# Attention in slots of four query blocks, with the value products of two groups in one block of the array

## The chip, the core and the metric

The kernel runs on one core of a Trainium2 chip. A core has five engines that run at the same time, each in its own program order, and wait for one another through semaphores: TensorE (PE) for matrix products, VectorE (DVE), ScalarE (ACT) and GpSimd (POOL) for elementwise work, and SyncE (SP), which here issues most of the DMA transfers. PE reads its operands from SBUF and writes its results to PSUM, a small memory of eight banks; the other engines copy results out of PSUM. PE works in two steps, a weight load (PEld in the profile) and the matmul that streams columns past the loaded weights.

The metric is the device time of one execution in microseconds (us): the median over repeated runs.

## The reference

The reference is one decoder layer on a sequence of 4096 positions of width 1024. After an RMS norm and an input projection, two groups of heads work side by side, and their gated outputs go through one output projection, a residual add and a last RMS norm. What matters here is the first group: eight heads of width 64, each with three branches of sliding-window attention on the same q, k, v.

```python
DILATED_BRANCHES = ((128, 1), (512, 4), (2048, 16))   # window, dilation
...
s = jnp.einsum('bhrnqd,bhrnkd->bhrnqk', qb, kb) * (Dh ** -0.5)
...
s = jnp.where(mask, s, jnp.finfo(jnp.float32).min)
m = jnp.max(s, axis=-1, keepdims=True)
p = jnp.exp(s - m)
den = jnp.sum(p, axis=-1, keepdims=True)
o = jnp.einsum('bhrnqk,bhrnkd->bhrnqd', p.astype(v.dtype), vb) / den
```

With dilation d the sequence falls into d residues r, and each residue into blocks n of 128 queries. A block attends to its own 128 keys and to the 128 before it (none before block 0). So every branch has 32 blocks of 128 queries: 32 of one residue in branch 0, 8 each of four residues in branch 1, 2 each of sixteen in branch 2. The second group of heads is a retention in 32 chunks of 128 positions (scores with a decay, outputs from a running state, a group norm per head).

## The kernel before

The kernel has three stages. Stage 1 projects q, k, v and the retention's q and k. Stage 2 (`phase2`, the stage that the change touches) does the attention, and beside it the retention with its own value projection. Stage 3 does the gates and the output projection.

All five engines run the order in which the program was written (`manual_schedule`). In stage 2 two generators are woven into one order.

`attention()` goes through 192 groups, 24 per head, each of four query blocks (`head_groups`, from L375). A group's two pairs of blocks are its two *banks*. For a bank:

- `qk_bank` (L598): S, the scores of two blocks against 256 keys each, in one PSUM bank; four matmuls. Two S banks exist (`psS`). For branches 1 and 2, `gather_q` (L579) first copies the queries of a group together, half on DVE and half on POOL, two groups ahead.
- `row_max` (L632): on DVE, mask and row minimum of one block, in place in the S bank. The scores carry a minus sign, so the minimum serves as the maximum.
- `exp_row` (L640): on ACT, the exponential of one block into P, with the row sum.
- `t_bank` (L647): four transposes of P on PE into T; `t_copy` (L658) copies T to `pt`, bank 0 by DVE and bank 1 by ACT.
- `pv_ops`, `pv_group` (L666, L673): O, the values. The weights are 128 keys x 64 value columns, so one product fills half of the array's columns. Bank 0 of the group goes to one half, bank 1 to the other, in turn, and the two halves run side by side. The result is 64 rows x 256 columns in either half of one PSUM bank.
- `o_copy` (L695): on ACT, O to SBUF; `store_o` (L713) stores it by SP.

The loop (L766) runs in half groups t: S of bank t, transposes of the bank two half steps back, O of a group at every even t, then the ACT and DVE work. `later` and `issue_due` put stores and loads some half steps on.

`filler()` (L969) yields the retention's work in small parts, each with an estimated cost in ns. A chunk's value projection V has eight parts (k from 0 to 7) of three matmuls; between them come the retention's scores Rs, the transposes Rk of the decayed keys, the outputs Ro in two halves, the transposes Rt of the normalised output, and the next state Rkv, whose products are 64 columns wide like O's. `group_norm` (L930) puts DVE's normalising work beside V's parts: statistics at k=0, aggregate at 1, and at 4 and 5 two heads each, read from the bank (`psG`) into which the next Ro goes. `split_rk` (L848) prepares the next chunk at k=7.

The loop at the end of `phase2` weaves: after each half step it takes filler parts until the sum of costs reaches what is due by then (`slot`), so that the filler lasts until some steps (`TAIL`) before the end of the attention. When all values of V are done, stage 3's weights are loaded and split beside the rest (`early3`). Stage 3 begins with the scaling of its first block of inputs (`split_h`, L432 to L440), which needs a transfer of `rs`.

## Time and profile before

| | |
|---|---|
| time, median of 3 runs | 2446.45 us (2445.19 to 2449.05) |
| the profiled execution, its own time | 2448.65 us |
| span of its trace, first to last instruction | 2446.9 us |
| PE clock granted, mean | 0.986 of full |
| stage 2 in the trace, first S to last O | about 778 to 1682 us |
| O's matmul instructions (two per product) | 1968 |
| HBM read and written | 241.18 MB, 118.64 MB |

A row of the timeline gives start, duration, engine, line, operation, the tiles (out<-in), their shapes, and how many instructions of one kind were merged; in brackets the idle time of the engine before it, with what ended it. PE's matmuls are pipelined: their durations overlap, so their cost is read from start to start. A row of the groups by line gives the count, then the busy time in all and the mean of one in ns, then the idle time before them. A row of the waits gives who waited for whom, the time in all, how often, and the longest.

### The profile page before, as it was taken

The numbers are of one execution on the slowest core, as the hardware profiler recorded it, in microseconds if no ns is written. First come the engines' busy times: TensorE is split into PE (matmuls) and PEld (weight loads), VectorE is DVE, ScalarE is ACT, GpSimd is POOL, SyncE is SP. The second block draws the span as 40 slices with busy tenths as digits, with TensorE's granted clock in tenths as the row PEclk, the third lists the DMA queues.
The fourth block names the chain that finished last, engine by engine and source line by source line (L and its number), as shares of the span: only waits on it lengthen the run. The fifth ranks groups of instructions, "written<-read, shape, count | busy, mean of one in ns | idle before, by whom it ended". The sixth has DMA issues, their size and how long they took to land.

```text
span 2446.9 us, 41800 instructions
## 1 busy us (share of the span) xinstructions
PE 2343.5 (96%) x14568; PEld 1985.9 (81%) x14568; DVE 1485.2 (61%) x3921; ACT 989.6 (40%) x2868; POOL 714.3 (29%) x761
## 2 busy tenths in 40 slices
PE   7999999999995999999999999996899999999998
PEld 5778888888884888887888887885889889999997
DVE  5643443444342878787777879786665565565554
ACT  4322212212212666666666666666222232232221
POOL 5312112112102535343444435354312112121110
PEclk9999999999997999999999999998999999999999
DMA  6343344343348565758576665746675656676663
GB/s 189 129 148 120 124 139 132 113 137 129 120 146 208 138 163 137 178 130 190 132 165 153 154 158 127 169 118 197 149 162 153 146 158 154 150 156 165 141 158 91
DMA packets 404067, 362.59 MB, mean 148 GB/s; under 512 B 191784, under 2 KB 334760, under 8 KB 398736
## 3 DMA queue, kind: packets, MB, share of 16 engines
q1 hardware_dynamic: 389216, 332.91, 52.5%
q10 hardware_dynamic: 14112, 25.43, 3.3%
q8 instruction: 115, 1.88, 0.3%
q0 software_dynamic: 528, 1.58, 0.2%
q14 instruction: 96, 0.79, 0.1%
HBM read 241.18 MB, written 118.64 MB: 147 GB/s over the span
## 4 chain that ended last, share of the span: by engine, by line
PE 74%; DMA 10%; DVE 5%; issue 2%; ACT 2%; POOL 2%; SPq 1%; ACTq 0%; POOLq 0%; DVEq 0%
PE S L615 8%; PE mm L49 8%; PE mm L50 8%; PE mm L51 8%; PE O L685 6%; PE T L652 5%; PE po L49 3%; PE po L50 3%; PE po L51 3%; PE g L50 3%; PE g L49 3%; PE g L51 3%; PE V L49 3%; DMA wb<-dr_w 2%; PE V L51 2%; PE V L50 2%
## 5 line engine op out<-in xcount | busy, mean ns | idle before, releaser
L636 DVE CUSTOM_DVE_ANT_0 S<-S,mask 128x256 f32<-128x256 f32 (+1 forms) x768 | 308.5, 402 | 168.7 <-PE S L615 139.1
L643 ACT ACTIVATE P<-S,nm 128x256 f32<-128x256 f32 (+1 forms) x768 | 337.4, 449 | 74.4 <-DVE nm L636 51.2
L51 PE MATMUL g<-h,wg 128*128 128x256 f32 x1024 | 290.6, 284 | 0.0
L652 PE MATMUL T<-ident,P 128*128 128x128 f32 x1368 | 213.3, 273 | 0.4 <-ACT P L643 0.4
L615 PE MATMUL S<-kk,qc 128*128 128x256 f32 x1024 | 186.5, 306 | 17.1 <-ACT P L643 11.8
L50 PE MATMUL po<-wo,m 128*128 128x512 f32 x512 | 201.7, 394 | 0.0
L51 PEld LDWEIGHTS g<-h,wg 128*128 128x128 f32 x1024 | 197.6, 193 | 0.1
L685 PE MATMUL O<-pt,v 128*64 128x128 f32 (+1 forms) x1968 | 196.0, 325 | 0.2 <-ACT pt L662 0.2
L615 PEld LDWEIGHTS S<-kk,qc 128*128 128x128 f32 x1024 | 149.8, 190 | 45.5 <-issue 28.9
L41 ACT ACTIVATE m<-e 128x256 fp32r<-128x256 f32 x128 | 53.3, 417 | 323.9 <-DVE e L1123 171.7
L405 POOL TENSOR_TENSOR hc<-hr,hc 128x512 fp32r<-128x512 f32 x64 | 85.9, 1343 | 319.3 <-ACT hc L404 249.4
L49 PE MATMUL po<-wohi,m 128*128 128x512 f32 x448 | 175.7, 392 | 2.1 <-DVE x L1170 2.1
L1177 POOL TENSOR_TENSOR rs<-v,mhalf 128x1 f32<-128x1 f32 x32 | 17.3, 541 | 549.2 <-DVE v L1175 549.2
L51 PE MATMUL po<-wohi,m 128*128 128x512 f32 x448 | 176.4, 394 | 0.0
L159 POOL TENSOR_TENSOR sq<-sq,sq 128x512 f32<-128x512 f32 x56 | 76.2, 1361 | 326.8 <-ACT sq L155 326.8
L685 PEld LDWEIGHTS O<-pt,v 128*64 128x64 f32 x1968 | 121.4, 136 | 60.7 <-issue 31.0
L652 PEld LDWEIGHTS T<-ident,P 128*128 128x128 f32 x1368 | 163.7, 141 | 1.1 <-ACT P L643 1.1
L49 PE MATMUL g<-h,wg1hi 128*128 128x256 f32 x512 | 146.5, 287 | 14.2 <-ACT h L439 14.2
L643 ACT ACTIVATION_READ_ACCUMULATOR P<-S,nm 128x1 f32 x768 | 158.0, 206 | 0.0
L50 PE MATMUL g<-h,wg1hi 128*128 128x256 f32 x512 | 148.9, 291 | 2.2 <-DVE h L440 1.7
L49 PE MATMUL g<-h,wg0hi 128*128 128x256 f32 x512 | 145.0, 283 | 4.7 <-ACT e L1116 4.7
L50 PE MATMUL g<-h,wg0hi 128*128 128x256 f32 x512 | 144.8, 283 | 0.0
(207 smaller groups left out, 6097.9 us busy)
## 6 DMA issues: line engine op xcount, KB each, us to landing
hr<-in_xT_dram SPq DMA_DIRECT2D x64, 512.0 KB
q<-dr_q SPq DMA_DIRECT2D x128, 256.0 KB
wb<-dr_w SPq DMA_DIRECT2D x128, 192.0 KB
o<-dr_o SPq DMA_DIRECT2D x192, 128.0 KB
v<-dr_v SPq DMA_DIRECT2D x94, 256.0 KB
xt<-in_xT_dram SPq DMA_DIRECT2D x64, 256.0 KB
dr_q<-hl SPq DMA_DIRECT2D x32, 512.0 KB
dr_k<-hl SPq DMA_DIRECT2D x32, 512.0 KB
```

The lines of the kernel that those rows point to most:

```text
L41: nc.scalar.activation(dst[:, 0], src, AF.Copy)
L49: nc.tensor.matmul(out, wh, xh, start=first and i == 0, stop=False)
L50: nc.tensor.matmul(out, wh, xl, start=False, stop=False)
L51: nc.tensor.matmul(out, wl, xh, start=False, stop=last and i == n - 1)
L159: nc.gpsimd.tensor_tensor(sums[b], sums[b], sq, ALU.add)
L405: nc.gpsimd.tensor_tensor(hc[:, :, 1, :], src, hc[:, :, 0, :].bitcast(F32), ALU.subtract)
L615: nc.tensor.matmul(s[:, j * 256 : (j + 1) * 256], qq[h, t, half][:, off : off + 128] if br == 0 else it["q"][:, t, i, :], rhs, start=(j == ...
L636: nc.vector.tensor_tensor_reduce(sv, sv, mask[:, it["br"], c0:256], 1.0, BIG, ALU.add, ALU.min, accum_out=nm[:, col : col + 1])
L643: nc.scalar.activation(it["P", i // 2][:, i % 2, c0:256], sv, AF.Exp, bias=nm[:, col : col + 1], scale=-1.0, accum_out=den[:, col : col + 1])
L652: nc.tensor.transpose(t[:, j * 128 : (j + 1) * 128], it["P", bank][:, j // 2, j % 2 * 128 : j % 2 * 128 + 128], ident)
L685: nc.tensor.matmul(o[64 * bank : 64 * bank + 64, c0 : c0 + 128 * m], vt[h, br, idx // 8][:, idx % 8, :], it["pt"][:, a : a + m, :].rearran ...
L1177: nc.gpsimd.tensor_tensor(rs, v, mhalf, ALU.pow)
```

## The change

The attention now runs in slots of a whole group. In a slot g the PE order is: S of both banks of group g; filler parts marked "r"; the transposes of both banks of group g-1; filler parts marked "f"; and in odd slots the values of two groups, g-3 and g-2, in one block. Each of the two groups takes one half of the array's columns, with all its four blocks (64 rows x 512 columns in the bank). `pv_ops` now lists for every key block one product that serves its own queries and the next block's, where both are in the group.

The filler marks its parts by kind: V and Rs are "r", the others "f". The weaving takes parts of a kind only at that kind's place in the slot, and stops when the next part is of the other kind.

On DVE the four row minima of a group come in a row, on ACT its four exponentials. The copies of O cover two groups, so their count halves and their width doubles, and the stores' too. In branch 2 a group holds two neighbouring residues in place of two that lie four apart. There is one more buffer of P (4 for 3) and of `pt` (3 for 2), and the buffers for O's copy are twice as wide. The costs with which the weaving plans are set anew, and `TAIL` counts groups.

```diff
-TAIL = 8
+TAIL = 4
...
-    for r in (0, 1, 2, 3, 8, 9, 10, 11):
-        g.append((2, [(r, 0), (r, 1), (r + 4, 0), (r + 4, 1)]))
+    for r in (0, 4, 2, 6, 8, 12, 10, 14):
+        g.append((2, [(r, 0), (r, 1), (r + 1, 0), (r + 1, 1)]))
...
-        pp = pool("p2p", 3)
+        pp = pool("p2p", 4)
...
-        PT = [c2.tile([128, 8, 128], F32, name=f"pt{i}") for i in range(2)]
+        PT = [c2.tile([128, 8, 128], F32, name=f"pt{i}") for i in range(3)]
...
-        def pv_ops(it, bank):
-
-            r, n = it["blocks"][2 * bank]
-            s0 = 4 * bank
-            ops = [(r, n, s0 + 1, 2, 0), (r, n + 1, s0 + 3, 1, 128)]
-            return ([(r, n - 1, s0, 1, 0)] if n > 0 else []) + ops
+        def pv_ops(it):
+
+            ops, blocks = [], it["blocks"]
+            for i, (r, n) in enumerate(blocks):
+                if n > 0 and (r, n - 1) not in blocks:
+                    ops.append((r, n - 1, 2 * i, 1, i * 128))
+                ops.append((r, n, 2 * i + 1, 2 if (r, n + 1) in blocks else 1, i * 128))
+            return ops
...
-            ops = [pv_ops(it, bank) for bank in range(2)]
+            ops = [pv_ops(it) for it in pair]
             for x in range(-max(map(len, ops)), 0):
-                for bank in range(2):
+                for half in range(2):
...
-                ob = osp.tile([128, 256], F32, tag="os", name="os2")
-                nc.scalar.activation(ob, it["O"][:, :256], AF.Copy)
+                ob = osp.tile([128, 512], F32, tag="os", name="os2")
+                nc.scalar.activation(ob, o, AF.Copy)
                 c0 = n * 128 if br == 0 else r * 1024 + n * 128
-                later(2, store_o, h, br, c0, 512, ob)
+                later(2, store_o, h, br, c0, 1024, ob)
...
+            for g in range(n + 5):
+                clock[0] = 2 * g
                 issue_due()
-                it, b = half(t)
...
+                it, i1, i2 = item(g), item(g - 1), item(g - 2)
+                pair = items[g - 3 : g - 1] if g % 2 and 3 <= g < n + 2 else None
+                done = items[g - 4 : g - 2] if g % 2 == 0 and 4 <= g < n + 3 else None
...
+                if item(g + 2):
+                    gather_q(item(g + 2))
+                if done:
+                    o_copy(done)
+                cost = 0
                 if it:
-                    qk_bank(it, b)
-                    cost += 436
...
+                    for b in range(2):
+                        qk_bank(it, b)
+                    cost += 1030
+                if i2 and i2["gi"] == len(groups) - 1:
+                    end_head(i2["h"])
+                    cost += 2 * TRN
+                if it:
+                    for i in range(4):
+                        row_max(it, i)
+                    for i in range(4):
+                        exp_row(it, i)
+                rest = pv_cost(pair[1]) if pair else 0
+                yield "r", cost, rest + (t_cost(i1) if i1 else 0)
+                clock[0] = 2 * g + 1
+                issue_due()
                 if i1:
-                    exp_row(i1, 2 * b1)
-                    exp_row(i1, 2 * b1 + 1)
...
+                    for b in range(2):
+                        t_bank(i1, b)
+                        t_copy(i1, b)
+                yield "f", t_cost(i1) if i1 else 0, rest
+                if pair:
+                    pv_groups(pair)
+                yield "", rest, 0
...
                 for k in range(KT):
+                    yield ("r", 700) if c < NCH else ("f", 0)
...
                     if mid and k == 1:
+                        yield "r", 654
                         scores(mid)
                         decayed_q(mid)
-                        yield 654
                     if mid and k == 3:
+                        yield "f", 2 * TRN
                         decayed_k(mid)
-                        yield 2 * TRN
...
                         if mid:
+                            yield "f", 872
                             outputs(mid, 0)
-                            yield 872
                         if old:
+                            yield "f", 4 * TRN
                             ret_out(c - 2, old)
-                            yield 4 * TRN
                 if mid:
+                    yield "f", 872
                     outputs(mid, 1)
-                    yield 872
+                    yield "f", 478
                     next_state(mid)
-                    yield 478
...
+        for kind, cost, rest in attention():
             total += cost
-            while not values_done and total < (t + 1) * slot:
-                total += next(fg)
+            if not kind:
+                g += 1
...
+                continue
+            while not values_done and feed.next[0] == kind and total + rest < (g + 1) * slot:
+                total += feed.do()
```

The planner's due cost per slot, `slot`, is worked out as before from the costs of a head's groups and of the chunks' parts; a part's cost is now added when the part is done.

More of the change, by code (lines that the diff above doesn't have):

```diff
@@ L594, in gather_q @@
                     for n in range(2):
-                        src = qq[h, part, n].rearrange("p (m r) -> p r m", r=16)[:, r : r + 5 : 4, :]
+                        src = qq[h, part, n].rearrange("p (m r) -> p r m", r=16)[:, r : r + 2, :]
                         (nc.vector if part else nc.gpsimd).tensor_copy(t[:, part, n : n + 3 : 2, :], src)
@@ L685, in pv_group @@
                     nc.tensor.matmul(
-                        o[64 * bank : 64 * bank + 64, c0 : c0 + 128 * m],
+                        o[64 * half : 64 * half + 64, c0 : c0 + 128 * m],
                         vt[h, br, idx // 8][:, idx % 8, :],
-                        it["pt"][:, a : a + m, :].rearrange("p a b -> p (a b)"),
-                        start=-x == len(ops[bank]),
+                        pair[half]["pt"][:, a : a + m, :].rearrange("p a b -> p (a b)"),
+                        start=-x == len(ops[half]),
                         stop=x == -1,
@@ L1008, in filler, with __init__, do @@
                         if mid:
+                            yield "f", 872
                             outputs(mid, 0)
-                            yield 872
                         if old:
+                            yield "f", 4 * TRN
                             ret_out(c - 2, old)
-                            yield 4 * TRN
                 if mid:
+                    yield "f", 872
                     outputs(mid, 1)
-                    yield 872
+                    yield "f", 478
                     next_state(mid)
-                    yield 478
-        per_head = sum(
-            872 + TRN * (8 - sum(it["blocks"][2 * i][1] == 0 for i in range(2))) + pv_cost(it) for it in items[: len(groups)]
-        )
-        n = 2 * len(items)
-        slot = H * per_head / n + (NCH * (8250.0 + 6 * TRN) - LEAD - REST) / (n - TAIL)
+        class Feed:
+            def __init__(self):
+                self.parts = filler()
+                self.next = next(self.parts)
+            def do(self):
+                cost = self.next[1]
+                self.next = next(self.parts, None)
+                return cost
+        per_head = sum(1030 + t_cost(it) + (pv_cost(it) if i % 2 else 0) for i, it in enumerate(items[: len(groups)]))
+        n = len(items)
+        slot = H * per_head / n + (NCH * (8 * 700.0 + 3530.0) - LEAD - REST) / (n - TAIL)
         ctx.enter_context(tc.manual_schedule(engines=ORDERED))
-        fg = filler()
+        feed = Feed()
         total = 0.0
         while total < LEAD:
-            total += next(fg)
+            total += feed.do()
         total = 0.0
         gates = None
-        for t, cost in enumerate(attention()):
+        g = 0
+        for kind, cost, rest in attention():
             total += cost
-            while not values_done and total < (t + 1) * slot:
-                total += next(fg)
+            if not kind:
+                g += 1
+                if g == n - 4:
+                    ahead["h3"] = load_x_block(nc, qp, io, 0, soon)
+                continue
+            while not values_done and feed.next[0] == kind and total + rest < (g + 1) * slot:
+                total += feed.do()
             if values_done:
@@ L1040, in phase2 @@
                 for _ in range(2):
-                    next(fg, None)
+                    if feed.next:
+                        feed.do()
                 next(gates, None)
-            if t == n - 7:
-                ahead["h3"] = load_x_block(nc, qp, io, 0, soon)
-        assert not list(fg) and not list(gates)
+        assert not feed.next and not list(gates)
 def phase3(tc, io, dr, out, ahead, raw, M):
```

65 lines of the change are left out of this document (20 added, 45 removed).

## The prediction

> **What bounds the kernel now.** I read the page's head first, then the busy time by windows, then the timeline of the attention stage engine by engine, and the list of waits last.
>
> ```profile
> span 2446.9 us, 41800 instructions
> PE 2343.5 (96%) x14568; PEld 1985.9 (81%) x14568; DVE 1485.2 (61%) x3921; ACT 989.6 (40%) x2868; POOL 714.3 (29%) x761
> PE 74%; DMA 10%; DVE 5%; issue 2%; ACT 2%; POOL 2%; SPq 1%; ACTq 0%; POOLq 0%; DVEq 0%
> ...
> 778.00:1682.00 904.00, 873.90 (x6799) 730.24 (x6799) 707.53 (x2573) 602.87 (x2071) 402.30 (x455) 0.99 0.64 153
> ```
>
> The last row, of the windows, gives the length, the busy time of PE, weight loads, DVE, ACT and POOL, and the granted clock (0.99). The changed stage runs from 778 to 1682, 904 us for 192 groups, 4.7 us each. PE is busy for 97% of it and leads the chain of waits, DVE for 78%. So the PE order decides, and DVE stands close behind. What a busy row hides is seen in the starts on PE:
>
> ```profile
> 902.34 0.63 PE L615 MATMUL S<-kk,q 128*128 128x256 f32 x4
> 902.81 0.60 PE L652 MATMUL T<-ident,P 128*128 128x128 f32 x4
> ...
> 903.94 0.64 PE L615 MATMUL S<-kk,q 128*128 128x256 f32 x4
> 904.41 0.60 PE L652 MATMUL T<-ident,P 128*128 128x128 f32 x4
> ...
> 907.83 0.40 PE L49 MATMUL V<-w2hi,hc 128*128 128x512 f32 x1
> ...
> 908.52 0.64 PE L615 MATMUL S<-kk,q 128*128 128x256 f32 x4
> 909.00 0.60 PE L652 MATMUL T<-ident,P 128*128 128x128 f32 x4
> 909.53 1.09 PE L685 MATMUL O<-pt,v 128*64 128x128 f32 x12
> ...
> 911.12 0.60 PE L652 MATMUL T<-ident,P 128*128 128x128 f32 x4
> ```
>
> From start to start: four S take 904.41 - 903.94 = 0.47 us (0.117 each); three V (two rows left out) take 908.52 - 907.83 = 0.69; four T and three V take 903.94 - 902.81 = 1.13, so four T 0.44, 0.109 for 128 columns. Between these kinds nothing is lost. With an O in between, 909.00 to 911.12 is 2.12 us for four T, twelve O and four S. The twelve O are six on either column half, side by side, and stream eight times 128 columns per half: 0.87 at the pace of T. What is left, 2.12 - 0.44 - 0.47 - 0.87 = **0.34 us**, is what going to the 64-column form (the 128*64 in the row) and back costs, once per group, 192 times.
>
> **The change, part by part.** *Values of two groups at once.* An O block now holds two groups, one per half. Columns per half double (1024 for two groups, where two blocks had 512 each), so the streaming is the same. The entries halve: 96 x 0.34 = **-32.6 us**. The next-state product Rkv has the 64-column form too:
>
> ```profile
> 922.30 0.66 PE L917 MATMUL Rkv<-vch,kd 128*64 128x128 f32 x8
> ...
> 923.47 0.60 PE L652 MATMUL T<-ident,P 128*128 128x128 f32 x4
> ```
>
> Four S stand between the two rows. 1.17 us less S 0.47 less four steps of 0.109 (two halves side by side) leaves 0.26 for the way out. Laying the filler's parts out with the diff's loop and its cost figures, I count 8 of 32 Rkv right before an O: 8 x 0.26 = **-2.1 us**.
>
> The O instructions fall from 1968 to 1712, since a block that serves two queries in one half is now read once. I cost this at nothing: the loads lie beside the streaming.
>
> ```profile
> L685 PEld LDWEIGHTS O<-pt,v 128*64 128x64 f32 x1968 | 121.4, 136 | 60.7 <-issue 31.0
> ```
>
> The Trainium skill, "TensorE: Matmul & The Clock Gate", section "The mechanism" of Part 3, says that weight loads overlap running matmuls only where the row group differs; here all use all 128 rows. By that rule 256 loads of 136 ns would go as well, up to 35 us more. The steps above speak against it: O, with a load before every matmul, is timed by its columns.
>
> *S, T by whole groups.* Between them the trace has no switch cost, so putting them together gains nothing on PE. It changes what PE must wait for. Before, two banks of S came half a step apart. Now both come at the start of a slot, four row minima follow on DVE, then four exponentials on ACT, and the second S bank of the next slot needs the fourth of them.
>
> ```profile
> 903.12 0.43 DVE L636 CUSTOM_DVE_ANT_0 S<-S,mask 128x256 f32<-128x256 f32 x1 [1.29 <-PE S L615]
> 903.64 0.43 DVE L636 CUSTOM_DVE_ANT_0 S<-S,mask 128x256 f32<-128x256 f32 x1
> 903.99 0.14 DVE L636 DVE_READ_ACCUMULATOR2_ANT nm<- 128x1 f32 x1
> 904.23 0.47 ACT L643 ACTIVATE P<-S,nm 128x256 f32<-128x256 f32 x1 [0.19 <-DVE nm L636]
> ...
> 905.60 0.69 DVE L664 COPY pt<-T 128x512 f32<-128x512 f32 x1
> 906.43 0.42 DVE L892 TENSOR_TENSOR kd<-Rk,kdec 128x256 f32<-128x256 f32 x1
> ```
>
> The first row minimum starts 903.12 - 902.34 = 0.78 after S; rows follow at 0.525 and the accumulator ends 0.49 after its row's start: four rows 2.07. The exponential starts 0.10 later and lasts 0.47. So the fourth ends at 3.42 after the slot's start at best, and 0.57 after the fourth row otherwise. The next second bank wants to start 0.47 into its slot: a slot under 2.95 us stalls PE, and a late DVE stalls longer ones. The other DVE work of a slot:
>
> ```profile
> 894.26 0.61 DVE L926 SCALAR_TENSOR_TENSOR state<-state,cdec,Rkv 128x128 f32<-128x128 f32 x2
> 894.78 0.88 DVE L941 BATCH_NORM_STATS2 bs<-Ro 128x6 f32<-128x128 f32 x4
> 895.59 0.36 DVE L944 BATCH_NORM_AGGREGATE mv<-bs 128x2 f32<-128x6 f32 x4
> 895.98 0.33 DVE L945 TENSOR_SCALAR rs<-mv 128x4 f32<-128x4 f32 x1
> ...
> 899.59 0.69 DVE L880 TENSOR_TENSOR stm<-Rs,decay 128x512 f32<-128x512 f32 x1
> ...
> 907.89 1.36 DVE L950 TENSOR_SCALAR on<-Ro,mv,rs 128x128 f32<-128x128 f32 x4
> 911.35 0.62 DVE L591 CAST qc<-q 128x512 fp32r<-128x512 f32 x1 [2.10 <-issue]
> ...
> 915.01 0.30 DVE L636 CUSTOM_DVE_ANT_0 S<-S,mask 128x128 f32<-128x128 f32 x1
> ...
> 918.02 1.01 DVE L591 CAST qc<-q 128x512 fp32r<-128x512 f32 x1
> ...
> 922.07 0.58 DVE L854 CAST qbd<-rq 64x256 fp32r<-64x256 f32 x2
> 922.68 0.29 DVE L855 CAST rkh<-rk 128x256 fp32r<-128x256 f32 x1
> ```
>
> I use: T copy 0.60 (0.69, the next starts 0.08 before its end), gather 0.62 and 1.01 in branch 2, statistics 0.81, aggregate 0.72, stm 0.69, normalising two heads 0.68, split 0.90, kd 0.42, state 0.61, four rows of branch 2 1.80 (two are 128 wide). PE parts: S 0.94, T 0.87, V 0.69, Rs 0.70, Rk 0.22, Ro half 0.89, Rt 0.44, Rkv 0.79, O of a pair 2.08 (1.65 in branch 2). Odd slots carry O; of the 93 even slots up to 186, 32 sum to under 3.0 us, since a filler part whose turn is in the other half of the slot blocks the rest. Sixteen slots laid out, in us from each slot's start. DVE's part after the rows goes by the V parts of a chunk (V0 statistics, V1 aggregate, V4 and V5 normalising, V7 split), then stm after Rs, the T copy, kd or state, and the next slot's gather; what is left over at the slot's end is the next row's DVE free. In slot 26 rows end at 2.85, copy 3.45, kd 3.87, gather 4.49, and 4.49 - 2.95 leaves 1.54.
>
> ```
> slot parts              PE   DVE free rows end exp end  PE stall
> 25 S V0-1 Rs V2 T O    6.66    0        2.85    3.42
> 26 S V3 T Rk           2.72    0        2.85    3.42   0.23 (S)
> 27 S V4-5 T O          5.27    1.54     3.71    4.28
> 28 S V6 T Ro Rt        3.83    1.02     3.19    3.76
> 29 S V7 T O            4.58    0.58     2.85    3.42
> 30 S T Ro Rkv          3.49    0.39     2.85    3.42
> 31 S V0-1 T O          5.27    1.23     3.40    3.97
> 32 S Rs V2-3 T Rk      4.11    0.88     3.05    3.62
> 33 S V4 T O            4.58    1.27     3.44    4.01
> 34 S V5-6 T Ro         4.08    1.15     3.32    3.89   0.81 (Ro)
> 35 S T Rt O            4.33    0.72     2.89    3.46
> 36 S V7 T Ro Rkv       4.18    0.17     2.58    3.15
> 37 S V0 T O            4.58    1.62     3.52    4.09
> 38 S V1 Rs V2-3 T      4.58    1.36     3.26    3.83
> 39 S T Rk O            3.68    1.70     3.60    4.17   0.02 (S)
> 40 S V4-6 T Ro Rt      5.21    1.95     3.85    4.42   1.33 (Ro)
> ```
>
> The Ro stalls are a new wait: Ro overwrites the bank that normalising reads, and where both fall in one slot (16 of 32 chunks) normalising stands behind four rows on DVE; queued behind Ro are T's followers, O and the next S. Sum 2.39 us in 16 slots, 0.15 each; over 186 slots **+27.8 us**. Against that, waits that the trace has already:
>
> ```profile
> PE S L615 <- ACT P L643: 13.8, 16, 2.4
> ...
> PEld S L615 <- ACT P L643: 6.2, 17, 1.5
> ```
>
> 20.0 us. The long ones (up to 2.4) begin where DVE's gather waits for its load, and stay. Between nothing and all I let half go: **-10 us**.
>
> *The rest at nothing.* One copy of O for two groups: 64 wide ones for 128 of branches 0 and 1, 32 for 64 in branch 2, off PE's path since ACT is 67% busy (602.87 of 904); should the strided one be twice as long, the row minima cover it. Stores of O by SP halve in number. The new order of branch 2 gathers the same elements, on DVE and on POOL, two groups ahead as before. At the stage's end, the last pair's O comes about 1 us later, beside a wait that lasts longer:
>
> ```profile
> 1691.46 7.12 POOL L438 TENSOR_TENSOR hr<-hr,rb 128x256 f32<-128x256 f32 x8 [8.88 <-DMA rb<-dr_rs]
> ```
>
> PE's first gate product hangs on this chain, and rb's load stands on SP behind the last stores of O, before and after. If that cover failed it would cost that 1 us.
>
> Sum: -32.6 - 2.1 + 27.8 - 10 = **-17 us**. The profiled execution took 2448.65 us, so 2431.7; it lay 2.2 us above the median of the runs (2446.45), so I forecast 2429.5.
>
> **The rivals.** *Full gain.* DVE runs ahead of my table, new stalls stay at the old 20 us: -34.7, 2412; with the old ones gone too, 2392. For it: DVE waits for S, as in the row at 903.12. Against: in the table it is the one that is late. 0.20.
>
> *DVE becomes the bound.* The table uses best prices. Its DVE sum is 68.5 us of 71.2. Adding 0.5 us of lag to every slot raises the sixteen slots' stalls to 4.24 us (26: 0.23, 32 before Rk: 0.35, 34: 1.31, 39: 0.52, 40: 1.83), +49 over the stage: net +5, within the measurement's grain. Adding 0.75 gives 5.5, +64: net +19, 2466. It decides at 0.45 us. For it: the gather that DVE got 2.10 us late at 911.35 already reached PE through the exponentials:
>
> ```profile
> 914.15 0.71 PE L615 MATMUL S<-kk,qc 128*128 128x256 f32 x4 [0.86 <-ACT P L643]
> ```
>
> Against: a third of the slots (branch 0) gather nothing, where my sample has three of sixteen. No change 0.13, slower 0.15.
>
> *The switch is not what costs.* If the 0.34 belonged to each group's own first loads it would double in a pair's block: no saving, +18, 2464. Against: V after T, and T after S, load weights too and pay nothing. 0.04.
>
> *Loads were exposed*, as the page's rule has it: 35 us more, 2394. 0.02.
>
> **How the numbers follow.** Forecast 2429.5 with 0.46 (its own range 2415 to 2441). Faster by over 0.2% (4.9 us, about what a measurement of this kernel can tell from no change): 0.46 + 0.20 + 0.02 = 0.68. Within it 0.13; slower 0.15 + 0.04 = 0.19. The range leaves out the best corner and the worse half of the slow cases: 2398 to 2460.
>
> **What would show it.** O x1712 in blocks of up to 20, 96 of them; "issue" idle before O's weight loads halved from 31.0 us; PE stalls before Ro and, after short even slots, before S, released by ACT or DVE; DVE's idle time before the row minima much smaller. I am wrong if PE's starts around O keep 0.34 per group, if stalls before S and Ro exceed 45 us, or if the end of the stage moves against the load of rb.

## The result and the profile after

The change makes the kernel slower, by 1.2%.

| | before | after |
|---|---|---|
| median, us | 2447.73 | 2477.47 |
| range of the runs, us | 2445.19 to 2449.05 | 2474.57 to 2478.92 |
| ratio after to before, 95% interval | | 1.0121, 1.0104 to 1.0139 |
| profiled execution, us (span) | 2448.65 (2446.9) | 2478.92 (2477.1) |

The before column holds one execution more than the table that stands ahead of the prediction. All ratios are of executions in the fast state, so one of e19_uneven's six, of 4581 us, is not in its ratio.

The forecast was 2429.5 us, faster; the measured time lies above its range. First the page of the kernel after: span, busy time by engine, the chain that ended last, and the weight loads of O (busy time and mean ns, then the idle time before them).

```profile
span 2477.1 us, 40841 instructions
...
PE 2336.6 (94%) x14312; PEld 1987.3 (80%) x14312; DVE 1485.4 (60%) x3921; ACT 984.5 (40%) x2772; POOL 721.7 (29%) x761
...
PE 72%; DMA 9%; DVE 6%; issue 4%; ACT 3%; POOL 2%; SPq 1%; ACTq 0%; DVEq 0%; POOLq 0%
...
L687 PEld LDWEIGHTS O<-pt,v 128*64 128x64 f32 x1712 | 113.9, 137 | 52.2 <-issue 11.7
```

O's instructions are the 1712 that were forecast, and "issue" idle time before their loads fell from 31.0 to 11.7 us. Busy times hardly moved: what was added is idle time. The windows of the kernel after (length, then busy time of PE, weight loads, DVE, ACT, POOL, the granted clock):

```profile
778.00:1720.00 942.00, 867.46 (x6543) 730.54 (x6543) 702.60 (x2571) 596.22 (x1975) 406.08 (x453) 0.97 0.62 149
```

From the first S to the last O the kernel before took 902.9 us and the kernel after 932.4, +29.5 of the +30.2 in all. The other pieces cancel: the start of the stage +5.2, the way from the last O to the first gate product +4.8 (11.8 to 16.6), the last stage -9.1 (753.7 to 744.6).

**Where the stage's time is.** I followed the starts on PE from 8 us after the first S to the last O, gave every block the pace of the prediction's first part, and every way into or out of the 64-column form what it takes before (0.15 in, 0.21 out). What a block starts later than that by more than 0.15 us is a wait, put down to the block that is late; "even" and "odd" are the groups' numbers. All in us:

| kernel | length | switches | S even | S odd | T | Ro | other waits | gaps under 0.15 |
|---|---|---|---|---|---|---|---|---|
| before | 893.3 | 78.0 | 20.0 | 10.0 | 10.5 | 0 | 1.0 | 13.1 |
| after | 921.3 | 42.6 | 34.1 | 36.9 | 18.4 | 6.7 | 10.0 | 12.4 |
| e12_early | 894.8 | 42.6 | 14.8 | 36.2 | 13.4 | 6.2 | 8.4 | 13.9 |
| e14_banks | 906.1 | 42.6 | 32.6 | 40.0 | 3.4 | 6.4 | 9.3 | 12.5 |
| e17_before_eo | 879.6 | 78.3 | 8.4 | 8.1 | 10.3 | 0.6 | 1.2 | 12.4 |
| e19_uneven | 873.9 | 42.6 | 6.1 | 37.0 | 6.6 | 4.0 | 8.1 | 10.5 |
| e15_even_early_banks | 870.2 | 45.1 | 13.9 | 8.6 | 6.7 | 13.1 | 14.1 | 9.5 |

The rest of each row is work, 759 to 761 us in all of them. So the saving came (78.0 to 42.6; since the small gaps did not grow, a switch costs what it did, and there are fewer), and waits of 41.5 us became 106. The starts say the same of the switch: from O's last product to the first of the next kind the median is 0.203 us in both kernels.

Two things in the table need care. T's 10.5 us before are some fifty steps of 0.15 to 0.2 us just over the bound, and the profile lists no wait of T from 800 to 1660 us there; after the change T waits up to 4 us. And blocks that run at half clock (last section) count as late too. Over the table's length they take 13.9 us more than the pace allows after the change, 2.5 before.

The waits that the profile lists for the kernel after, from 800 to 1660 us (us in total, times, longest):

```profile
PE S L615 <- ACT P L643: 22.7, 38, 6.2
PEld S L615 <- ACT P L643: 21.0, 54, 1.0
...
PE T L652 <- DVE pt L664: 11.8, 7, 3.8
...
PE S L615 <- DMA q<-dr_q: 8.7, 3, 3.9
...
PE Ro L914 <- DVE on L958: 1.1, 3, 0.5
```

The new waits stand before S and T. Ro, to which the prediction gave nine tenths of the new stalls, hardly waits.

### The profile page after: what moved, and what is told of

Its sections match the earlier page's. It is cut to its first block, busy times and chain, and to the rows that moved or that the text cites. A ratio compares the mean times of both kernels' runs of the same rounds, so it can differ in the third digit from the quotient of the medians.

```text
span 2477.1 us, 40841 instructions
## 1 busy us (share of the span) xinstructions
PE 2336.6 (94%) x14312; PEld 1987.3 (80%) x14312; DVE 1485.4 (60%) x3921; ACT 984.5 (40%) x2772; POOL 721.7 (29%) x761
## 4 chain that ended last, share of the span: by engine, by line
PE 72%; DMA 9%; DVE 6%; issue 4%; ACT 3%; POOL 2%; SPq 1%; ACTq 0%; DVEq 0%; POOLq 0%
PE mm L49 8%; PE mm L50 8%; PE mm L51 8%; PE S L615 6%; PE po L50 4%; PE po L51 4%; PE po L49 4%; PE O L687 4%; PE g L50 4%; PE g L49 4%; PE g L51 4%; PE T L652 4%; DMA q<-dr_q 3%; ACT P L643 2%; PE V L51 2%
## 5 line engine op out<-in xcount | busy, mean ns | idle before, releaser
L636 DVE CUSTOM_DVE_ANT_0 S<-S,mask 128x256 f32<-128x256 f32 (+1 forms) x768 | 300.5, 410 | 188.4 <-PE S L615 136.3
L615 PE MATMUL S<-kk,qc 128*128 128x256 f32 x1024 | 175.3, 312 | 25.9 <-ACT P L643 16.9
L652 PE MATMUL T<-ident,P 128*128 128x128 f32 x1368 | 186.5, 277 | 12.6 <-DVE pt L664 12.6
L615 PEld LDWEIGHTS S<-kk,qc 128*128 128x128 f32 x1024 | 141.3, 194 | 49.4 <-issue 27.8
L687 PE MATMUL O<-pt,v 128*64 128x256 f32 (+1 forms) x1712 | 174.2, 343 | 0.0
L687 PEld LDWEIGHTS O<-pt,v 128*64 128x64 f32 x1712 | 113.9, 137 | 52.2 <-issue 11.7
L643 ACT ACTIVATION_READ_ACCUMULATOR P<-S,nm 128x1 f32 x768 | 152.9, 199 | 0.0
```

The costliest lines, as they stand in the source:

```text
L615: nc.tensor.matmul(s[:, j * 256 : (j + 1) * 256], qq[h, t, half][:, off : off + 128] if br == 0 else it["q"][:, t, i, :], rhs, start=(j == ...
L636: nc.vector.tensor_tensor_reduce(sv, sv, mask[:, it["br"], c0:256], 1.0, BIG, ALU.add, ALU.min, accum_out=nm[:, col : col + 1])
L643: nc.scalar.activation(it["P", i // 2][:, i % 2, c0:256], sv, AF.Exp, bias=nm[:, col : col + 1], scale=-1.0, accum_out=den[:, col : col + 1])
L652: nc.tensor.transpose(t[:, j * 128 : (j + 1) * 128], it["P", bank][:, j // 2, j % 2 * 128 : j % 2 * 128 + 128], ident)
L687: nc.tensor.matmul(o[64 * half : 64 * half + 64, c0 : c0 + 128 * m], vt[h, br, idx // 8][:, idx % 8, :], pair[half]["pt"][:, a : a + m, :] ...
```

## The experiments

The theory on record says that the switch is saved and new stalls take back half. It fell, so the runs ask for each new wait where it comes from. Each time stands as a ratio to the kernel before, run on the same chip.

### The halves of the change

*e3_pair_alone*: the half steps of before, with O in pairs (and the new order of branch 2 and third `pt`, which the pairs use).

```diff
-                g = (t - 4) // 2 if t % 2 == 0 else -1
+                g = (t - 6) // 2 if t % 4 == 2 else -1
...
-                    pv_group(items[g])
+                    pv_groups(items[g : g + 2])
```

> The kernel before, in half steps as it was, with only the values of two groups in one block (one O in four half steps). Theory S (the switch to the 64-column form costs 0.34 us each time): 96 entries fewer, about 33 us less than before, 2414. If the switch is not what costs: no change, 2447. If a burst of O of twice the length starves DVE and ACT: some of the 33 us is given back, 2420 to 2440.

*e4_slots_alone*: the slots of after, with one group's O in each (and branch 2 in its old order).

```diff
-                pair = items[g - 3 : g - 1] if g % 2 and 3 <= g < n + 2 else None
+                pair = items[g - 2] if 2 <= g < n + 2 else None
```

> The changed kernel without the pairs: slots of four query blocks, but the values of one group in every slot. Theory S: 96 entries more than the changed kernel, about 33 us more, 2510. If the slots' uneven length (O in odd ones) is what costs, the even slots give time back: 2450 to 2490.

Measured: 1.0018 (1.0002 to 1.0035) and 1.0025 (1.0011 to 1.0040). The pairs alone save the switches (45.5 us of them left) and give it all back in waits (79.3 us in all, 41.0 of them before S in even groups); the time lies above all that was expected of it. The slots alone keep 68.7 us of switches and are still 1% faster than the whole change: S in odd groups waits 10.7 us there, not 36.9. So neither half alone is the whole loss, and the two losses of 0.2% do not add up to it.

### SP's queue

The longest wait of the stage, in the kernel after, three engines in order of time:

```profile
812.73 0.61 DVE L591 CAST qc<-q 128x512 fp32r<-128x512 f32 x1 [8.60 <-DMA q<-dr_q]
...
814.36 0.47 ACT L643 ACTIVATE P<-S,nm 128x256 f32<-128x256 f32 x1 [9.50 <-DVE nm L636]
...
815.53 1.19 PE L615 MATMUL S<-kk,qc 128*128 128x256 f32 x4 [6.22 <-ACT P L643]
```

DVE's gather waits for q with four row minima behind it; the exponentials wait for these and S for the exponentials. Why q is late, the SP queue's own timeline tells:

```profile
787.88 1.81 SPq L548 DMA_DIRECT2D q<-dr_q  x4
800.98 0.40 SPq L396 DMA_DIRECT2D hr<-in_xT_dram  x1
801.42 1.97 SPq L548 DMA_DIRECT2D q<-dr_q  x4
```

Four of the head's eight loads of q stand 11 us behind the load of hr, whose buffer POOL must free first by its split (hc). SP's waits there, after:

```profile
SPq L396 <- POOL hc L405: 182.7, 29, 11.1
```

and before:

```profile
SPq L396 <- POOL hc L405: 40.5, 19, 6.9
```

The half of a chunk that POOL splits last is asked for behind the first V part and the next load behind the third; with V parts put together these often fall into one slot, and ACT's part of the split stands behind four exponentials. Three ways to take this apart. *e1_hr_pool*: POOL issues that load.

```diff
-                        hraw[c + 1] = load_x_chunk(nc, hcp, io, c + 1)
+                        hraw[c + 1] = load_x_chunk(nc, hcp, io, c + 1, nc.gpsimd.dma_start)
```

> The changed kernel, with the load of the retention's input chunk (hr, L396) issued by POOL in place of SP. Theory Q (queue): SP stands 183 us behind POOL's split of hr (40 us before), so the loads of q behind it land late, DVE's gather waits in front of the row minima, PE runs dry and its clock is halved: SP's wait at L396 goes, the PE gaps of over 1 us shrink from 51 us to 25 or less, the time falls by 25 to 45 us, to about 2440. Theory D (lag of DVE behind four rows and the planner's short slots): the gaps over 1 us have another cause, the time falls by at most 5 us, to about 2473.

*e2_gather_late*: the gather behind the row minima and the exponentials of its slot.

> The changed kernel, with the gather of the queries written after the slot's row minima and exponentials in place of ahead of them. Theory Q: a late load of q no longer holds the rows of the running slot, only the S two slots on; the loads are as late as before, so part of the long gaps stays: 10 to 20 us less, about 2462. Theory D: DVE's rows start by up to 1 us earlier in most slots with a gather, the short waits before S (0.3 to 1 us) go as well: also about 10 to 20 us less, but in the short gaps, with the long ones left.

*e12_early*: the split moved forward, SP keeps the load.

```diff
-                    if k == 0 and 1 <= c < NCH:
-                        hch[c].append(split_h_chunk(nc, hcp, hraw.pop(c), c, 1))
...
+                    if k == HS + 1 and c < NCH - 1:
+                        hch[c + 1].append(split_h_chunk(nc, hcp, hraw.pop(c + 1), c + 1, 1))
```

> The changed kernel with the second half of a chunk of x split (ACT, POOL) right after the first, at the seventh V of the chunk before, not behind the first V of its own. The buffer of hr is then free some six V parts before SP comes to its next load, and SP, not POOL, issues it. Theory Q (SP's queue standing at that load makes q late, DVE's gather waits for q in front of the row minima): SP's wait there falls from 183 us to under 40, the waits over 1 us on PE from 45 to about 28 as with the load on POOL, and the time to 2455 to 2462. If the waits over 1 us stay above 40, the queue is not their cause.

Measured: e1_hr_pool 1.0022 (1.0005 to 1.0038); e2_gather_late 1.0097 (1.0074 to 1.0120), a miss: S even falls to 18.5 us, and T (23.8) and Ro (13.1) wait in its place; e12_early 1.0007 (0.9994 to 1.0020). With the split moved, SP's longest class of wait at the load is

```profile
SPq L396 <- POOL qbd L867: 3.6, 4, 1.2
```

and S even falls from 34.1 to 14.8 us. Two edits that have only the freed queue in common give 1.0% and 1.1%: the queue is some 25 us of the loss. *e8_before_hr* and *e7_pair_hr* are e1's edit on the kernel before and on e3_pair_alone.

> The kernel before with the hr load issued by POOL, a control: SP stands 40 us at that load there, against 183 after the change. Theory Q: what the queue costs before is small, 0 to 8 us off, 2440 to 2448. If it falls by over 10 us, the queue was a cost of the kernel before as well, and what the run e1_hr_pool gained was not the change's own loss.

> The kernel of the run e3_pair_alone (half steps of before, O in pairs) with the hr load issued by POOL. Theory Q: the waits over 1 us there, 37.6 us, come in part from SP's queue standing at the hr load; they fall to about 25 and the time to about 2445. Rival: they come from S waiting on the exponentials because of DVE's order in half steps; then the time stays at 2455 to 2460.

Measured: 1.0011 (0.9996 to 1.0027), so the kernel before gains nothing when POOL issues the load. ACT's wait for hr grows from 4.2 to 11.2 us in that run, so it does not price the queue by itself. And 1.0166 (1.0142 to 1.0189), much worse than e3_pair_alone. The waits of e7_pair_hr point to the cause:

```profile
PE S L615 <- ACT P L643: 47.1, 33, 7.1
...
ACT hc L404 <- DMA hr<-in_xT_dram: 36.9, 12, 4.9
```

POOL issues the load late, and now ACT stands in front of its split with the exponentials behind it (12.2 us of that in e3_pair_alone). As these rows have it, the wait was moved from SP's queue to ACT, which is nearer to PE; in the changed kernel, moving the split (1.0007) does no worse than moving the load (1.0022). The Trainium skill, "SBUF — State Buffer", section "SBUF: two separate sides", warns that a DMA issued by POOL can stall for its descriptors while DVE copies; no run here tells that apart from POOL's own order.

### T's banks

T waits for DVE's copy in a way that the code does not ask for. In the kernel after:

```profile
1535.78 0.60 PE L652 MATMUL T<-ident,P 128*128 128x128 f32 x4
...
1539.44 0.69 DVE L664 COPY pt<-T 128x512 f32<-128x512 f32 x1
...
1540.18 0.66 PE L652 MATMUL T<-ident,P 128*128 128x128 f32 x4 [3.81 <-DVE pt L664]
```

The second half of a group waits until DVE has copied the first half, as if there were one bank and not two. In the built program that is so: 41 of 392 T tiles lie in the bank of the tile just before them, none in the kernel before. The tiles are handed the bank that comes free first in the order in which the program is laid out, and the new order puts ACT's copy of the older tile behind. *e14_banks* fixes one bank for each half:

```diff
-            t = psT.tile([128, 512], F32, tag="T", name="T2")
+            t = psT.tile([128, 512], F32, tag=f"T{bank}", name="T2")
```

> The changed kernel with the two PSUM banks of T fixed by half (first half always in one, second in the other; the planner's allocator put 41 of 392 T tiles into the bank of the tile just before). Theory B: T's waits for DVE's copy, 18 us (7 of them 1.7 to 4 us), fall to under 5, and the time to 2458 to 2465. Rival: the wait only moves to the S behind it, which needs exponentials that stand behind the same row minima; then 2470 or more.

Measured: 1.0060 (1.0040 to 1.0080); T's waits 18.4 to 3.4 us. So T's banks are some 15 us, or 0.6%, a little less than expected.

### Short slots

S in odd groups, the largest new wait, with a short even slot in the kernel after:

```profile
1024.93 1.21 PE L615 MATMUL S<-kk,q 128*128 128x256 f32 x8
...
1025.82 0.30 DVE L636 CUSTOM_DVE_ANT_0 S<-S,mask 128x128 f32<-128x128 f32 x1 [2.55 <-PE S L615]
...
1026.21 0.43 DVE L636 CUSTOM_DVE_ANT_0 S<-S,mask 128x256 f32<-128x256 f32 x1
1026.56 0.14 DVE L636 DVE_READ_ACCUMULATOR2_ANT nm<- 128x1 f32 x1
...
1026.82 0.37 ACT L643 ACTIVATE P<-S,nm 128x128 f32<-128x128 f32 x1 [1.17 <-DVE nm L636]
...
1027.47 0.14 DVE L636 DVE_READ_ACCUMULATOR2_ANT nm<- 128x1 f32 x1
...
1027.70 0.47 ACT L643 ACTIVATE P<-S,nm 128x256 f32<-128x256 f32 x1
...
1027.78 0.74 PE L615 MATMUL S<-kk,q 128*128 128x256 f32 x4 [0.18 <-ACT P L643]
...
1028.16 0.47 ACT L643 ACTIVATE P<-S,nm 128x256 f32<-128x256 f32 x1
...
1028.78 0.74 PE L615 MATMUL S<-kk,q 128*128 128x256 f32 x4 [0.25 <-ACT P L643]
```

The first exponential (1026.82) starts not behind the first row minimum but behind the second, which began at 1026.21 and whose accumulator ends at 1026.70. The third (1027.70) starts behind the fourth row, whose accumulator ends at 1027.61. The fourth ends at 1028.63, 1.02 after that and 3.70 after the slot's start, and S's second bank starts 0.15 later. It is so in all 192 slots: neither the first nor the third exponential starts less than 0.03 us behind the second and the fourth accumulator, and the fourth ends 1.02 us behind the latter (median; 0.94 to 1.31). Over the even slots of the stage the median start of the first exponential is 1.98 us into the slot; with four full rows at 0.46 the fourth ends at 3.83. S's second bank wants to start 0.47 into the next slot, so a slot under about 3.40 us stalls. By the parts' lengths of the prediction, the 93 even slots lack 32.5 us of that; 26.9 were added. *e5_even* drops the rule that ties a filler part to its place:

```diff
-            while not values_done and feed.next[0] == kind and total + rest < (g + 1) * slot:
+            while not values_done and total + rest < (g + 1) * slot:
```

> The changed kernel, with the planner free to put a filler part at either place of a slot, whatever its kind. By the diff's cost figures and the measured lengths of the parts, the even slots grow from 3.45 us to 4.28 on average and the odd ones, which carry the O of a pair, fall from 5.21 to 4.39; 32 even slots under 3.0 us become none. Theory U (the short even slots make S wait in the odd slot behind them): the waits of 0.15 to 1 us on PE in the attention stage fall from 58 us to 25 or less, the time to about 2445. The waits over 1 us (45 us, SP's queue standing at the hr load) stay. Theory D (DVE and the chain from S through DVE and ACT back to S are too slow on average, whatever the lengths of the slots): the waits stay above 50 us, the time at 2465 to 2480.

*e6_even_hr* is both this and e1's edit.

> The same, and the hr load issued by POOL as in the run e1_hr_pool. Theory U, with theory Q for the waits over 1 us (SP's queue): both effects add, 17 us and some 30 us off 2477, about 2430, faster than before. Theory D: no better than e1_hr_pool, 2460.

Measured: 1.0127 (1.0106 to 1.0148) and 1.0078 (1.0055 to 1.0101). S odd falls from 36.9 to 7.9 us in e5_even as the theory says, but S even rises to 42.7, T to 21.8 and Ro to 13.4: nothing is gained, and the times of both runs are those of theory D (e1_hr_pool, whose edit e6_even_hr holds, stands at 1.0022 without e5's). Where the pieces lie matters to who waits, not yet to how long. So the 26.9 us of S odd are a wait that the trace shows, and not time that comes back when it goes.

### DVE's own load

The rival on record was that DVE has no room. *e9_direct* has no gathers: S loads its weights from q where it lies.

```diff
-                        qq[h, t, half][:, off : off + 128] if br == 0 else it["q"][:, t, i, :],
+                        w[t],
```

> The changed kernel without the gathers: in branches 1 and 2 the weight loads of S read q where it lies, every 4th or 16th element, so neither DVE nor POOL copies anything and the wait for q's load moves from DVE, two groups ahead, to S. Theory D (in the slots of branches 1 and 2, DVE with its gathers has no room: a slot is planned at 4.2 us, DVE's work in one is about 4.4): the groups of branches 1 and 2 fall from 4.69 and 4.74 us to 4.5 or less, the waits of 0.15 to 1 us on PE from 58 to 30, and with the gather's waits for q the time falls to about 2435. Theory L (the waits come from the loop S, DVE, ACT, S itself, not from what else DVE does): under 10 us less, 2467 or more. A strided weight load may itself be slower than the 136 ns of a packed one; then S shows it in its own lines and the run says nothing on D.

*e11_quarter* and *e18_quarter_even* cut DVE's share of the gather to a quarter, in the changed kernel and in the best version below.

```diff
-                    (nc.vector if part else nc.gpsimd).tensor_copy(t[:, part].rearrange("p b j -> p (b j)"), src)
+                    w = 128 if part else 512
+                    (nc.vector if part else nc.gpsimd).tensor_copy(t[:, part].rearrange("p b j -> p (b j)")[:, :w], src[:, :w])
```

> The changed kernel with DVE's share of the gather cut to the first quarter of each block; the other three quarters of those weights are left out (they stay at zero), POOL's share is whole. DVE's wait for q stays where it is. By the means of 0.76 and 1.20 us a gather, DVE loses some 80 us of work over 128 groups. Theory D: the waits of 0.15 to 1 us fall from 58 to 35 or less, the groups of branches 1 and 2 get 0.15 to 0.25 us shorter, the time 2445 to 2455. Theory L: the time stays within 8 us of 2477.

> The run e15_even_early_banks with DVE's share of the gather cut to the first quarter of each block; the other three quarters of those weights are left out (they stay at zero), POOL's share is whole. Theory D (DVE's gather, up to 1.9 us beside POOL's, stands in front of the row minima): the groups of branch 2 fall from 4.66 to 4.45 us or less, those of branch 1 from 4.43 to 4.35, the time to 2410 to 2420. Rival: POOL's share, or the loop through the exponentials, holds branch 2; within 6 us of e15_even_early_banks.

Measured: e9_direct 1.0346 (1.0307 to 1.0384). It says nothing on DVE, as its expectation allowed: with every 4th or 16th element read, the weight loads of S take longer and are no longer hidden: its products follow each other at 0.23 us in branches 1 and 2, where they did at 0.12 to 0.14 (medians). The loads of all three branches (duration of one: minimum, median, maximum):

```profile
L614 PEld LDWEIGHTS S<-kk,q x1536: 186/310/338, 781.3 to 1758.7; 128*128 128x128 f32 x192
```

against those of branches 1 and 2 in the kernel after, packed:

```profile
L615 PEld LDWEIGHTS S<-kk,qc x1024: 186/189/337, 815.5 to 1682.8; 128*128 128x128 f32 x171
```

The 136 ns in the expectation are a load of O's; S's packed loads take 189.

e11_quarter: 1.0051 (1.0034 to 1.0068). DVE loses 47 us of gathers (121.3 to 74.3), not 80, and the kernel gains 0.7%, but not where the theory has it: the groups of branch 2 go from 4.74 to 4.69 us, those of branch 1 from 4.69 to 4.66, and S odd stays at 34.7. The time lies between the two theories. e18_quarter_even: 0.9887 (0.9858 to 0.9916), 0.2% below the version it is made from, with intervals that overlap, and branch 2 stays at 4.64 us a group (4.66). The 47 us of DVE's work that these runs take away are not what holds the stage; more of it was not taken away. What holds branch 2 at 4.64 to 4.66 while the last groups of branch 0 run at 4.33 stays open.

### What the change is worth when its new waits are gone

*e13_even_early_order*: e5_even with the split of e12_early, and with branch 1 in the order of q's halves, so that the half loaded last is asked for three slots later (the stores of branch 1 follow that order).

```diff
-    for r in range(4):
-        for n in (0, 4):
+    for n in (0, 4):
+        for r in range(4):
```

> The run e5_even (filler parts free to stand at either place of a slot) with the early split of e12_early, and with branch 1 in the order of q's halves: its four groups on the first half of the columns, then the four on the second, so that the second half of q, loaded from the head's first slot on, is asked for three slots later. In every head of every run so far S waits longest at the head's fifth group, the first of branch 1. Theory Q+U: the first groups of a head fall from 5.1 to 5.6 us to about 4.4, the waits over 1 us to under 20 us, and the time to 2425 to 2440, less than before. Theory L (the loop S, DVE, ACT, S alone sets the pace): the gain of the one place is lost at the next; the time stays at 2460 or above.

*e15_even_early_banks* adds the fixed T banks; *e16_late* puts e15's gather behind the row minima; *e19_uneven* is e15 with the diff's rule for filler parts back; *e17_before_eo* is the kernel before with the early split and the order of branch 1.

> The run e13_even_early_order with T's banks fixed (there 50 of 392 T tiles share the bank of the one before, and T waits 22 us). Theory B: T's waits go, time 2433 to 2440, below the kernel before by 0.4% or more. Rival: S waits in T's place; 2450 or more.

> The run e15_even_early_banks with a group's gather put behind the row minima and exponentials of its slot on DVE and POOL. A gather of branch 2 takes 0.67 us on DVE alone and up to 1.9 beside POOL's; in front of the row minima it delays all four exponentials. Theory O (this order is what is left of S's waits): the waits of S fall by 8 us or more and the time to 2425 to 2433. Rival (as in the run e2_gather_late): the later gather only makes T's copy late instead; within 5 us of e15_even_early_banks.

> The run e15_even_early_banks with the diff's own rule back (a filler part only at the place of its kind), so that even slots are short again; early split, order of branch 1 and fixed T banks stay. Theory U: the fourth exponential ends 3.8 us after its slot's start, the second S bank of the next slot wants to start 0.47 into it, so a slot under 3.40 us stalls PE; the planned even slots lack 32.5 us in all. S's waits in odd slots are 30 to 35 us again and the time 2455 to 2463, 24 to 32 above e15_even_early_banks. Rival: without the late q, hr and T the chain has slack enough; 2440 or less.

> The kernel before with the early split of hr and branch 1 in the order of q's halves, a control. SP stands 40 us at the hr load there, and S waits 1.0 to 2.6 us at the first group of branch 1 in every head, 12 us in all. Theory Q as the change's own loss: at most these 12 us go, 2436 to 2447. If the time falls by 20 us, the two repairs are worth as much without the change, and the change is to be compared with that.

| run | median, us | ratio to before | 95% interval |
|---|---|---|---|
| e13_even_early_order | 2453.32 | 0.9997 | 0.9980 to 1.0013 |
| e15_even_early_banks | 2431.58 | 0.9910 | 0.9890 to 0.9930 |
| e16_late | 2434.44 | 0.9925 | 0.9905 to 0.9946 |
| e19_uneven | 2433.95 | 0.9930 | 0.9905 to 0.9955 |
| e17_before_eo | 2437.44 | 0.9940 | 0.9921 to 0.9958 |

e15_even_early_banks beats both kernels, by 0.9% and (from the two ratios to before) 2.1%. e13_even_early_order missed its 2425 to 2440 us. The page of e15_even_early_banks:

```profile
span 2424.6 us, 40846 instructions
...
PE 81%; DVE 5%; DMA 5%; issue 2%; ACT 2%; SPq 1%; POOL 0%; ACTq 0%; DVEq 0%; POOLq 0%
```

PE leads the chain for 81% of the span, where it was 74% before and 72% after, and DMA for 5% against 9%. Three things follow. The control e17_before_eo gains 0.6% without the change: the early split and the order together are worth some 12 us of S even in the kernel before as well (20.0 to 8.4); which of the two does it wasn't tried. Beside that control, e15_even_early_banks is 0.3% faster, with intervals that overlap, so most of the 0.9% is not the change's. And e19_uneven, which is the change with its queue, order and banks repaired, is 0.1% faster, within the intervals: 35.7 us of switches saved, 28.9 us of S odd and 6.9 of other waits to pay. Last, the expectation of e19_uneven was half right: S odd is there as priced (37.0 us), but the time is the rival's (2440 or less). Taking it away, as e15_even_early_banks does, gave 0.2%, not 24 us: S even, Ro and the other waits take up 23 of its 28 us and the mixed order has 2.5 us more switches. e16_late is the second miss of a later gather.

## Why the prediction was wrong, point by point

*The switch (-32.6 and -2.1)* was right: 35.4 us fewer, at an unchanged price. The rival that the switch isn't what costs falls with it.

*Loads hidden, at nothing*: right. O has 256 loads fewer, and the small gaps (13.1 to 12.4 us) leave no room for a gain from them.

*New stalls (+27.8)*: wrong in both parts, and near in total by luck. S odd added 26.9 us and Ro 6.7, 33.6 together, where the prediction's table gives S 2.9 and Ro 24.9 over the stage: two errors of opposite sign. For S, the sentence "So the fourth ends at 3.42 after the slot's start at best" comes from letting each exponential follow its own row, 0.10 behind its accumulator. The rows it used show otherwise: the exponential at 904.23 stands 0.10 behind the end of the accumulator that started at 903.99, and that is the second row's. The third follows the fourth row in the same way, so the fourth ends 1.02 us behind that row, not 0.57. That moves the limit for a slot from 2.95 to 3.40 us. The sample adds to the error: the plan's 93 even slots lack 16.8 us by the prediction's own limit, where its sixteen slots gave 0.25, or 2.9 for the stage; by 3.40 they lack 32.5, and 26.9 were measured. For Ro, DVE was less late than the column "DVE free" said: its idle time before the row minima, which was to become much smaller, went from 168.7 to 188.4 us.

*Old waits (-10)*: **the step that failed.** "The long ones (up to 2.4) begin where DVE's gather waits for its load, and stay", and half of the 20 us was to go. None of them went. S even rose from 20.0 to 34.1 us, its longest wait from 2.4 to 6.2, and T's row from 10.5 to 18.4, with waits for its copy that the kernel before does not have: +22.0 where -10 was forecast, 32 of the 45 us by which the stage missed. Two mechanisms make them that the prediction doesn't have. One is SP's queue at the load of hr, though the load and its split are issued by the very filler parts that the change puts together (*The rest at nothing* priced the stores of O in that queue, not the loads). The other is T's banks, which can't be read from the diff, only from the program it builds. Repairing the queue alone gives back 1.0 or 1.1% (S even 14.8 us in e12_early), the banks alone 0.6% (T 3.4). Both, with the order of branch 1 (e19_uneven), give back 1.9% while S odd keeps its 37 us; of that, the split and the order give the kernel before 0.6% too. The 9.0 us of other waits, at nothing in the sum, are not explained.

*End of the stage (1 us, hidden)*: it moved by 4.8 us against the load of rb, the last of the prediction's own signs of being wrong. The last stage's 9.1 us less cover it, in all runs with slots (744.6 to 748.9 against 753.7); why that stage is shorter wasn't tried. Another of these signs came as well: the stalls before S and Ro, named as over 45 us, are 77.7.

*DVE becomes the bound* was the rival on the right side, 2466 us, but not the mechanism as far as the runs show: e11_quarter and e18_quarter_even take 47 us of DVE's work away, and the waits of the stage fall by some 11 and 2 us. The sum of measured terms for the stage: -35.4 of switches, +26.9 S odd, +14.1 S even, +7.9 T, +6.7 Ro, +9.0 other waits, -1.2 for small gaps and the rest: +28.0, the growth of the table's length.

## What to carry to other kernels

A saving on the busiest engine arrives only if everything that feeds it has slack in the new order; a wait that is there already can grow, so ask what makes it. Price the loop of waits from one product to its own next turn with the trace's starts (which row an instruction really stands behind), over all slots and not a sample. When parts are put together, follow every load and buffer release that they issue: here one load that waits for a buffer held up the whole queue behind it, and an automatic choice of banks turned two buffers into one. Repair the waits on the kernel before as well, or the change is credited with what the repair gave.

## What was not expected of the hardware

The clock follows the gaps. Windows of the kernel after, from its longest S wait on, from another of 4.3 us, and from one of 1.7; the granted clock is the third value from the right:

```profile
815.00:824.00 9.00, 8.47 (x45) 7.93 (x46) 5.76 (x21) 5.75 (x20) 3.38 (x3) 0.65 0.48 118
824.90:831.70 6.80, 6.36 (x57) 4.99 (x56) 5.30 (x18) 4.65 (x16) 4.75 (x5) 1.00 0.46 108
932.00:940.90 8.90, 8.49 (x48) 7.95 (x49) 7.06 (x24) 6.17 (x21) 3.91 (x3) 0.70 0.31 73
...
1381.00:1384.40 3.40, 3.40 (x18) 3.40 (x18) 2.79 (x9) 2.94 (x11) 1.10 (x1) 0.50 0.52 122
```

V's products at half clock (817) and at full (822), and the third of these waits:

```profile
817.37 0.63 PE L49 MATMUL V<-w2hi,hc 128*128 128x512 f32 x1
817.80 0.63 PE L50 MATMUL V<-w,hc 128*128 128x512 f32 x1
...
822.64 0.39 PE L49 MATMUL V<-w2hi,hc 128*128 128x512 f32 x1
822.87 0.40 PE L50 MATMUL V<-w,hc 128*128 128x512 f32 x1
...
1379.78 1.68 PE L615 MATMUL S<-kk,qc 128*128 128x256 f32 x8 [1.67 <-ACT P L643]
```

Behind S waits of 6.2 us (the row at 815.53) and 4.3 us (by the starts) the clock averaged 0.65 and 0.70 over 9 us; then, in the second row, 1.00. From 800 to 1700 us it stood at half for 30.7 us after the change and for 3.4 before. That is not free: V's products follow each other at 0.43 us at half clock and at 0.23 at full, and these stretches make up most of the 13.9 us named below the table. How much shorter the kernel would be without them no run shows, since PE might then wait sooner for the exponentials. The Trainium skill, "TensorE: Matmul & The Clock Gate", section "Part 1: The HAM clock gate", puts the idle window that halves the clock at about 3.4 us. The first two waits are longer; but behind 1.67 us (the row at 1379.78) the clock was at half for 3.4 us too, and behind 1.73 us at 967.89 it was not, so the length of the wait before it does not settle it here.

DVE's gather of branch 2 takes 0.67 us for two when POOL is idle and 1.89 beside POOL's split and copies, in e13_even_early_order:

```profile
1386.12 1.29 POOL L405 TENSOR_TENSOR hc<-hr,hc 128x512 fp32r<-128x512 f32 x1 [6.45 <-ACT hc L404]
1386.47 1.89 DVE L596 CAST qc<-q 128x256 fp32r<-128x256 f32 x2
...
1387.35 2.59 POOL L596 CAST qc<-q 128x256 fp32r<-128x256 f32 x4
...
1390.66 0.67 DVE L596 CAST qc<-q 128x256 fp32r<-128x256 f32 x2
```

The Trainium skill, "SBUF — State Buffer", section "SBUF: two separate sides", has DVE and POOL share a pair of ports that one of them holds for a whole instruction; the rows fit that. Its mean over the stage moved little (538 to 602 ns), and as e18_quarter_even shows it did not decide the time.
